# A two-layer trunk kernel on one core: some weight tiles of layer 0 go into the matmul as loaded, in float32

## The chip, the core and the metric

The kernel runs on 1 core of one Trainium2 chip. The metric is the device time in microseconds (us) of one execution; the median of 3 runs of the kernel before is 559.33 us (558.77 to 559.34). Float32 data reaches TensorE in two forms here: as `float32` (called plain below), and as `float32r`, a rounded form. The kernel gets its precision from pairs of `float32r` tiles: a tile `hi` that holds the rounded value and a tile `lo` that holds the rest.

## The reference, cut to what matters

Input: 256 tokens of width 1024, float32. Each of two layers computes

```
h = rmsnorm(x, pre_g) * (1 + scale) + shift      # scale, shift, gate from silu(c) @ ada_w + ada_b
y = concat(branch_i(h) * silu(z_i)) @ out_w
x = x + gate * rmsnorm(y, post_g)
```

In layer 0 `h @ in_w` gives z (2048 columns), the channels of a state space branch (SSD, behind a causal convolution of 4 taps), 16 step sizes, and q, k, v of 16 attention heads. The output projection takes 2048 rows of weights to 1024 columns. Layer 1 has the same frame with other branches. The change touches two places of layer 0: the products of h with the weights of z, and the last 256 of the 2048 rows of the output projection.

## The kernel before, in words

Weights come in units of 1 MB, 128 x 2048 values, in the order that `stream_order` (L42) writes down: eight pieces of modulation, between them seven units called x (the convolution channels and the first unit of z), then for layer 0 seven more units of z, 4 of v, 8 of qk and 8 of the output projection. Behind z1, z3, z5 and z7 stands one more 1 MB piece each (a "gate" piece, consumed by VectorE into `acc`); pieces of the next layer's modulation stand behind some units of qk and of the output projection.

A unit lands in one of 3 buffers called `raw`. Each of its halves (128 x 1024) is split by `next_half` (L900): ScalarE writes `whi`, and VectorE or, where the planner prefers it, GpSimd writes `wlo = raw - whi`. There are 4 buffers of each. After both splits `raw` is free for the next load. `proj_cm` (L921) multiplies a half in three terms of 8 matmuls, 256 columns wide: hi by hi, hi by lo, lo by hi, against `hhi` and `hlo`, the two parts of h. So a half of z is 24 matmuls, a unit 48.

`hhi` and `hlo` come from `xnT`, which holds h in plain float32 after `h0_rows` (L1289) has modulated it in place. `xnT` lies in the only buffer of tag `D`; in the kernel before nobody reads it after that, and the next tiles in that buffer are `dtw_` (L1342, work space for the step sizes, 16 partitions by 7 rows), then `vt` (v of layer 0), then others.

While the z units are multiplied, other engines work on what stands beside them: the convolution (`conv`: ScalarE and VectorE), softplus of the step sizes, the SSD branch (`cb_group`, `x_tokens`, `ssd`), and the gate pieces.

`out_proj` (L995) goes over 16 row tiles r of 128 rows. Row tile r takes half of a weight unit and the matching activation tile, which `ysplit` (L990) has split into `yh` and `yl` for two row tiles at a time; these lie in tag `r2`, which has 5 buffers of 512 columns. Each row tile makes 3 terms by 2 column parts of 512, for the token half m = 0, and the same again for m = 1. For r below `FIRST_HELD` (10) both halves follow each other; from r = 10 on the m = 1 products are kept for later ("held"), so that `residual(0, 0, ...)` (L1029) can begin when all rows of m = 0 are done, and its result feed `make_h1` (L961) and the first three v units of layer 1, which are multiplied half by half (`NV = 3`). Held rows 10 and 11, and the two halves of the first v unit, have their split tiles in buffers of tag `A` (11 buffers of 1024 columns) in place of `whi` and `wlo`.

The order of the work is not the order of the source. `Plan` records every operation, and `schedule` (L502) simulates a list of priorities with cost figures of its own and tries 120 variations with a fixed random seed; `issue` then emits the best order found, for all engines. Each engine executes its own instructions in that order. A changed operation can therefore change the order of operations far from it. Since all operations are emitted by one helper, the profile puts them all on one line, L535, and they are told apart by their tiles: `mm<-hhi,whi` is a product of a half's hi tile with hhi.

Of the kernel before, what the change touches and what calls it, by code (L numbers as in the profile page):

```python
# [15 lines left out]
SEQ = 256  # L16
DM = 1024
KT = 8
# [599 lines left out]
def trunk(ctx, tc, par, s5par, x, w, dtw, fw, postg, gateb, out):  # L618
    nc = tc.nc
    plan = Plan()  # L620
    V, A, G, T, S = (plan.engine(n, e) for n, e in (
        ("DVE", nc.vector), ("ACT", nc.scalar), ("POOL", nc.gpsimd), ("PE", nc.tensor), ("SP", nc.sync)))
# [5 lines left out]
    def const(shape, name, dt=F32):  # L628
        return plan.fixed(sb.tile(shape, dt, name=name))
# [14 lines left out]
    def shaped(t, shape):  # L644
        n = 1
        for d in shape[1:]:
            n *= d
        t = t[0:shape[0], 0:n]
        if len(shape) == 3:
            t = t.rearrange("p (a b) -> p a b", b=shape[2])  # L650
        elif len(shape) == 4:
            t = t.rearrange("p (a b c) -> p a b c", b=shape[2], c=shape[3])
        return t

    def tmp(tag, shape):
        return shaped(plan.new(tags[tag]), shape)

    def rows_of():

        made = {}  # L660

        def row(i, n=None):
            q, j = divmod(i, 4)
            if q not in made:
                made[q] = tmp("A", [P, 4, SEQ])
            return made[q][:, j, :] if n is None else made[q][:, j:j + n, :]
        return row

    def tmp_rounded():
        return plan.new(tags["A"], R32, tags["whi"].slots[0])  # L670

    def bank(tag):
        return plan.new(banks[tag])
# [28 lines left out]
    def pc(name, a=0, b=None):  # L702
        lo, hi = PCOLS[name]
        return pt[:, lo + a:(hi if b is None else lo + b)]
# [42 lines left out]
    for n in range(2):  # L747
        k, pb = slice(4 * n, 4 * n + 4), bank("st")
# [19 lines left out]
    def softplus(xb, tmps):  # L768

        e, s, s2, p = tmps  # L770
        V.scalar_tensor_tensor(e, xb, -1.0, xb, op0=ALU.mult, op1=ALU.min)
        A.activation(e, e, AF.Exp)
        V.tensor_scalar(s2, e, 2.0, None, op0=ALU.add)
        V.reciprocal(s2, s2)
        V.tensor_mul(s, e, s2)
        V.tensor_mul(s2, s, s)
        V.tensor_scalar(p, s2, 1.0 / 15.0, None, op0=ALU.mult)
        for c in (13, 11, 9, 7, 5, 3):
            V.scalar_tensor_tensor(p, p, 1.0 / c, s2, op0=ALU.add, op1=ALU.mult)
        V.scalar_tensor_tensor(p, p, 1.0, s, op0=ALU.add, op1=ALU.mult)  # L780
        V.tensor_scalar(e, xb, 0.0, None, op0=ALU.max)
        V.scalar_tensor_tensor(e, p, 2.0, e, op0=ALU.mult, op1=ALU.add)
        return e

    def split(src, hi, lo, lo_eng=None):
        A.activation(hi, src, AF.Copy)
        if lo_eng:
            lo_eng.tensor_sub(lo, src, hi.bitcast(F32))
        else:
            sub2(lo, src, hi.bitcast(F32))  # L790
# [60 lines left out]
    at = [0, 0]  # L851
# [18 lines left out]
    def modulation(i):  # L870

        while stream[i][0] in ("mod", "gate"):
            if i not in modulated:
                modulated.add(i)
                kind, l, c, *kh = stream[i]
                if kind == "mod":
                    if l == 0:
                        plan.rank = c - 500.0
                    modulate(l, c, load(i)[0:2])
                    if l == 0:  # L880
                        h0_rows(c)
                    plan.rank = None
                else:
                    ada_piece(l, c, kh[0], load(i)[2])
                    if kh[0] == 1:
                        ada_done(l, c)
            i += 1
        return i

    def raw_half():  # L890
        if at[1] == 0:
            raw_half.halves = load(at[0])
        return raw_half.halves[at[1]]

    def step():
        at[1] += 1
        if at[1] == 2:
            at[0], at[1] = at[0] + 1, 0

    def next_half(kdim, spare=False):  # L900

        at[0] = modulation(at[0])
        hi, lo = (tmp_rounded(), tmp_rounded()) if spare else (tmp("whi", [P, 1024]), tmp("wlo", [P, 1024]))
        it = stream[at[0]]
        split(raw_half(), hi, lo, G if it[0] == "x" and 2 * it[1] + at[1] in POOL_X else None)
        step()
        return [t.rearrange("p (k n) -> p k n", k=kdim) for t in (hi, lo)]

    def mm3(o, terms, first=True, last=True, **kw):

        for t, pairs in enumerate(terms):
            with plan.together():
                for j, (a, b) in enumerate(pairs):
                    T.matmul(o, a, b, start=first and t == 0 and j == 0,
                             stop=last and t == 2 and j == len(pairs) - 1, **kw)

    def by_terms(s_hi, s_lo, m_hi, m_lo, ks):

        return [[(a(k), b(k)) for k in ks] for a, b in ((s_hi, m_hi), (s_hi, m_lo), (s_lo, m_hi))]

    def proj_cm(done):  # L921

        pb = bank("mm").rearrange("p (m t) -> p m t", m=2)
        for m in range(2):
            hi, lo = next_half(KT)
            mm3(pb[:, m, :], by_terms(*(lambda k, t=t: t[:, k, :] for t in (hi, lo, hhi, hlo)), range(KT)))
        done(pb)
# [62 lines left out]
    def ysplit(ysrc):  # L990
        yh, yl = tmp("r2", [P, 2, SEQ]), tmp("r2", [P, 2, SEQ])
        split(ysrc, yh, yl)
        return yh, yl

    def out_proj(l, ytile):  # L995


        acc = [[bank("mm"), bank("mm")], [bank("mm"), bank("mm")]]
        ys = {}

        def rows(r, hl, m, parts=((0, 512), (512, 1024))):
            hi, lo = hl
            yh, yl = ys[r // 2]
            c = slice(P * m, P * m + P)
            for t, (a, b) in enumerate(((yh, hi), (yh, lo), (yl, hi))):
                with plan.together():
                    for c0, c1 in parts:
                        n, o = divmod(c0, 512)
                        T.matmul(acc[m][n][:, o:o + c1 - c0], a[:, r % 2, c], b[:, 0, c0:c1],
                                 start=(r == 0 and t == 0), stop=(r == 15 and t == 2), skip_group_check=True)  # L1010


        held, first = {}, FIRST_HELD[l]
        for r in range(16):
            if r % 2 == 0:
                ys[r // 2] = ysplit(ytile(r // 2))
            hl = next_half(1, l == 0 and r in HELD_A)
            rows(r, hl, 0)
            if r < first:
                rows(r, hl, 1)  # L1020
            else:
                held[r] = hl
        x0 = residual(l, 0, acc[0])
        for c in ((0, 512), (512, 1024)):
            for r in range(first, 16):
                rows(r, held[r], 1, (c,))
        return x0, residual(l, 1, acc[1])
# [100 lines left out]
    def silu_to(dst):  # L1128
        def done(pb):
            A.activation(dst, pb, AF.Silu)  # L1130
        return done
# [126 lines left out]
    xnT = tmp("D", [P, KT, SEQ])  # L1258
    for m in range(2):
# [8 lines left out]
        for q in range(2):  # L1268
# [3 lines left out]
            pb = bank("st")  # L1272
            with plan.together():
                for j in range(4):
                    k = 4 * q + j
# [5 lines left out]
    for i, n in enumerate(NWARM2):  # L1281
        m, q = divmod(i, 2)
# [35 lines left out]
    zs = rows_of()  # L1318
    for n in range(14):
# [3 lines left out]
        hi, lo = next_half(8)  # L1323

        for run in ([[0, 1], [2, 3], [4, 5], [6, 7]] if n >= 12 else [range(8)]):
            for t, (a, b) in enumerate(((hi, hhi), (hi, hlo), (lo, hhi))):
                with plan.together():
                    for j in run:
                        k, c = items[j]
                        T.matmul(xb6[c // 2][:, c % 2, :], a[:, j, :], b[:, k, :],  # L1330
                                 start=(k == 0 and c % 2 == 0 and t == 0), stop=(k == 7 and t == 2),
                                 skip_group_check=True)
# [6 lines left out]


    pdt = proj_small(0, "st")
    dtw_ = tmp("D", [16, 7, SEQ])  # L1342
    xb, adtT = dtw_[:, 0, :], dtw_[:, 5:7, :]
    aneg = const([16, 1], "aneg")
    A.activation(xb, pdt[1], AF.Copy)
    V.scalar_tensor_tensor(xb, pdt[0], pc("dtb")[0:16], xb, op0=ALU.add, op1=ALU.add)
    A.activation(aneg, pc("alog")[0:16], AF.Exp)
    spv = softplus(xb, [dtw_[:, n, :] for n in range(1, 5)])
    V.tensor_copy(adtT[:, 0, :], spv)
    V.tensor_scalar(adtT[:, 1, :], spv, aneg, -1.0, op0=ALU.mult, op1=ALU.mult)  # L1350
    dtk = const([P, 2, 2, 16], "dtk")
# [113 lines left out]
            5: [lambda: ssd(0)], 7: [lambda: ssd(1)], 9: [lambda: ssd(2)], 11: [lambda: ssd(3)]}  # L1465
    for i in range(8):
        if i:
            proj_cm(silu_to(zs(2 * i, 2)))
        for f in side.get(i, ()):
            f()  # L1470
    for i in range(4):
# [5 lines left out]
    for i in range(8):  # L1477
        proj_cm(qkdone(i, vt, zs(8 + i)))
        if i == 0:
            ssd_norm()  # L1480
            s5_prepare()
# [9 lines left out]
    for m in range(2):  # L1491
        make_h1(m, xns[m])
        c = slice(P * m, P * m + P)
        for n in range(NV):
            for t, kh in ((0, 0), (1, 0), (0, 1), (1, 1), (2, 0), (2, 1)):
                if (n, kh) not in vw:
                    vw[n, kh] = next_half(4, 2 * n + kh in V_A)
                h, w_ = ((hhi, 0), (hhi, 1), (hlo, 0))[t]
                with plan.together():
                    for k in range(4):  # L1500
                        T.matmul(vb[n][:, m, :], h[:, 4 * kh + k, c], vw[n, kh][w_][:, k, :],
                                 start=(m == 0 and t == 0 and kh == 0 and k == 0), stop=(t == 2 and kh == 1 and k == 3),
                                 skip_group_check=True)
# [18 lines left out]
    xb = ft[:, 0, :]  # L1522
# [3 lines left out]
    spv = softplus(xb, [ft[:, n, :] for n in range(1, 5)])  # L1526
# [134 lines left out]


FIRST_HELD = (10, 12)
HELD_A, V_A = (10, 11), (0, 1)

NWARM = 14
# [104 lines left out]
```

## Time and profile before

| | before |
|---|---|
| median of 3 runs | 559.33 us |
| the profiled execution's own time | 557.83 us |
| its span (first to last instruction) | 556.1 us |
| mean granted TensorE clock | 0.974 |
| busy: TensorE, VectorE, ScalarE, GpSimd | 521.6, 480.5, 366.9, 99.2 us |

A busy time is the sum of the instructions' records. A matmul's record is longer than what it costs in a row of matmuls, since they are pipelined: two records overlap. So what a matmul costs is read from the distance between starts, and an idle stretch is only the time in which no record runs. The granted clock is given as a share of 2.4 GHz; 0.5 would be 1.2 GHz.

### The profile page before, as it was taken

The page shows a single profiled execution, that of the slowest core. Times are in us where ns is not written, and L with a number is a line of the kernel's source. Part 1 is how long each engine was busy: PE and PEld are TensorE (multiplying, and loading weights), DVE is VectorE, ACT ScalarE, POOL GpSimd, SP SyncE. Part 2 cuts the span into 40 slices and gives each one's busy share as a digit, 9 for nine tenths or more (in the row PEclk, how much of TensorE's full clock was granted, in tenths as well). Part 3 has the DMA queues.
Part 4 walks back from the last instruction along what each step waited for, and adds up shares of the span by engine and source line. Part 5 has one row for each costly group of instructions (what it writes and reads, how often), then busy time and mean ns, then how long its engine had stood idle before and what let it go on. Part 6 is the DMA issues. An engine that isn't in the chain of part 4 may idle for free.

```text
span 556.1 us, 10554 instructions
## 1 busy us (share of the span) xinstructions
PE 521.6 (94%) x3996; PEld 467.7 (84%) x3996; DVE 480.5 (86%) x1077; ACT 366.9 (66%) x761; POOL 99.2 (18%) x97
## 2 busy tenths in 40 slices
PE   6999889899999999999599999999999879999995
PEld 4899878899989897778499998999989648887784
DVE  7898899999999999884947989999999775977974
ACT  5644883776576787555746477676767877877731
POOL 5300213224043000004200101112254410000000
PEclk9899989999999999999799999999999969999999
DMA  8999428457442277886305263335454310374812
GB/s 308 410 407 366 154 81 289 161 187 269 152 147 83 82 303 299 314 324 268 151 1 210 94 246 136 150 102 203 162 188 159 122 55 1 99 265 170 331 48 75
DMA packets 18626, 105.27 MB, mean 189 GB/s; under 512 B 2064, under 2 KB 2704, under 8 KB 8336
## 3 DMA queue, kind: packets, MB, share of 16 engines
q1 hardware_dynamic: 18576, 104.60, 50.7%
q8 instruction: 31, 0.51, 0.4%
q14 instruction: 19, 0.16, 0.1%
HBM read 103.55 MB, written 1.05 MB: 188 GB/s over the span
## 4 chain that ended last, share of the span: by engine, by line
PE 68%; DVE 17%; ACT 8%; issue 4%; DMA 1%; SPq 0%; POOLq 0%; POOL 0%; DVEq 0%; ACTq 0%
PE mm L535 52%; PE st L535 11%; PE y L535 5%; DVE b L535 5%; DVE wlo L535 4%; ACT whi L535 3%; DVE st L535 2%; ACT b L535 2%; DVE a L535 2%; DMA A<-in_w_dram 1%; DVE tb L535 1%; ACT A L535 1%; ACT L535 1%; ACT a L535 1%; DVE acc L535 1%
## 5 line engine op out<-in xcount | busy, mean ns | idle before, releaser
L535 ACT ACTIVATE whi<-raw 128x1024 fp32r<-128x1024 f32 x124 | 128.5, 1054 | 60.9 <-PE mm L535 47.1
L535 DVE TENSOR_TENSOR wlo<-raw,whi 128x1024 fp32r<-128x1024 f32 x107 | 132.1, 1246 | 21.1 <-ACT whi L535 20.8
L535 PE MATMUL mm<-hhi,whi 128*128 128x256 f32 x664 | 94.1, 282 | 5.0 <-ACT whi L535 4.0
L535 PE MATMUL mm<-hlo,whi 128*128 128x256 f32 x664 | 93.7, 281 | 0.0
L535 PE MATMUL mm<-hhi,wlo 128*128 128x256 f32 x656 | 93.0, 282 | 0.0
L535 PEld LDWEIGHTS mm<-hhi,whi 128*128 128x128 f32 x664 | 84.4, 189 | 7.6 <-ACT whi L535 4.7
L535 PEld LDWEIGHTS mm<-hlo,whi 128*128 128x128 f32 x664 | 84.2, 188 | 2.8 <-issue 2.5
L535 PEld LDWEIGHTS mm<-hhi,wlo 128*128 128x128 f32 x656 | 83.0, 188 | 3.3 <-issue 3.1
L535 ACT ACTIVATE b<-b,s 128x128 f32<-128x128 f32 (+1 forms) x160 | 65.8, 446 | 18.6 <-DVE s L535 18.2
L535 PE MATMUL mm<-whi,r 128*128 128x512 f32 x240 | 67.7, 394 | 0.0
L535 POOL TENSOR_TENSOR wlo<-raw,whi 128x1024 fp32r<-128x1024 f32 x17 | 41.6, 2455 | 102.9 <-ACT whi L535 97.1
L535 PEld LDWEIGHTS mm<-whi,r 128*128 128x128 f32 x240 | 44.3, 188 | 10.1 <-issue 1.2
L535 ACT ACTIVATE b<-tb,s5r 128x64 f32<-128x64 f32 (+3 forms) x128 | 41.0, 383 | 7.2 <-DVE tb L535 5.0
L535 PE MATMUL mm<-wlo,r 128*128 128x512 f32 x120 | 38.9, 394 | 0.6 <-DVE wlo L535 0.6
L535 DVE CUSTOM_DVE_ANT_0 raw<-raw,condb 128x1024 f32<-128x1024 f32 x32 | 38.2, 1217 | 0.4 <-DMA raw<-in_w_dram 0.4
L535 POOL TENSOR_TENSOR s<-s,nhalf 128x1 f32<-128x1 f32 (+1 forms) x9 | 7.8, 863 | 109.0 <-DVE s L535 107.1
L535 PEld LDWEIGHTS mm<-wlo,r 128*128 128x128 f32 x120 | 22.1, 188 | 5.8 <-DVE wlo L535 1.0
L535 DVE CUSTOM_DVE_ANT_0 b<-st,amask 128x128 f32<-128x128 f32 (+1 forms) x80 | 24.1, 351 | 1.6 <-PE st L535 1.4
L535 ACT ACT_TABLE_LOAD x16 | 20.5, 1283 | 6.0 <-DVE a L535 4.9
L535 DVE TENSOR_TENSOR tb<-b 128x16 f32<-128x16 f32 (+3 forms) x110 | 19.9, 219 | 4.3 <-ACT b L535 3.8
L535 PE MATMUL mm<-wlo,hhi 128*128 128x256 f32 x144 | 23.2, 283 | 0.1
L535 PE MATMUL mm<-whi,hhi 128*128 128x256 f32 x144 | 23.0, 281 | 0.0
(238 smaller groups left out, 896.7 us busy)
## 6 DMA issues: line engine op xcount, KB each, us to landing
raw<-in_w_dram SPq DMA_DIRECT2D x80, 1024.0 KB, 4.9
raw<-in_w_dram SPq DMA_DIRECT2D x16, 512.0 KB, 10.2
A<-in_w_dram SPq DMA_DIRECT2D x14, 512.0 KB, 10.2
xres<-in_x_dram SPq DMA_DIRECT2D x2, 512.0 KB, 4.3
b<-in_gateb_dram SPq DMA_DIRECT2D x4, 256.0 KB, 6.2
b<-in_postg_dram SPq DMA_DIRECT2D x4, 256.0 KB, 6.2
out_dram<-xres SPq DMA_DIRECT2D x3, 256.0 KB, 2.0
A<-in_s5par_dram SPq DMA_DIRECT2D x1, 512.0 KB, 5.7
```

The lines of the kernel that those rows point to most:

```text
L535: getattr(self.engines[e], method)(*[at(v) for v in a], **{n: at(v) for n, v in k.items()})
```

## The change

For z units 1, 3, 5 and 7 (`PLAIN_Z`), `proj_cm` gets h in plain float32 and takes the weights from `raw` without a split: one term of 8 float32 matmuls for a half. `raw` is read by the matmuls themselves, and so is in use until they end; `xnT` is in use until z7 is done. For row tiles 14 and 15 of layer 0 (`PLAIN`, the entry 16 leaves layer 1 as it was), `out_proj` takes the activation tile without `ysplit`, the weights from `raw`, and one term. `dtw_` moves to two buffers of tag `A`.

```diff
+    def raw_next():
+
+        at[0] = modulation(at[0])
+        r = raw_half()
+        step()
+        return r
...
-    def proj_cm(done):
+    def proj_cm(done, h=None):
...
+            if h is not None:
+                wt = raw_next().rearrange("p (k n) -> p k n", k=KT)
+                with plan.together():
+                    for k in range(KT):
+                        T.matmul(pb[:, m, :], wt[:, k, :], h[:, k, :], start=(k == 0), stop=(k == KT - 1))
+                continue
...
-            hi, lo = hl
-            yh, yl = ys[r // 2]
             c = slice(P * m, P * m + P)
-            for t, (a, b) in enumerate(((yh, hi), (yh, lo), (yl, hi))):
+            if r >= PLAIN[l]:
+                terms = ((ys[r // 2], hl[:, None, :]),)
+            else:
+                (yh, yl), (hi, lo) = ys[r // 2], hl
+                terms = ((yh, hi), (yh, lo), (yl, hi))
+            for t, (a, b) in enumerate(terms):
...
-                ys[r // 2] = ysplit(ytile(r // 2))
-            hl = next_half(1, l == 0 and r in HELD_A)
+                ys[r // 2] = ytile(r // 2) if r >= PLAIN[l] else ysplit(ytile(r // 2))
+            hl = raw_next() if r >= PLAIN[l] else next_half(1, l == 0 and r in HELD_A)
...
-    dtw_ = tmp("D", [16, 7, SEQ])
-    xb, adtT = dtw_[:, 0, :], dtw_[:, 5:7, :]
+    dtw_ = [tmp("A", [16, 4, SEQ]) for _ in range(2)]
+    xb, adtT = dtw_[0][:, 0, :], dtw_[1][:, 1:3, :]
...
-            proj_cm(silu_to(zs(2 * i, 2)))
+            proj_cm(silu_to(zs(2 * i, 2)), xnT if i in PLAIN_Z else None)
...
+PLAIN_Z = (1, 3, 5, 7)
+PLAIN = (14, 16)
```

## Rows read from the trace of the kernel before

**Rows 1.** The table of stretches, one row each (from two such tables): stretch, length, then busy time and count of PE, PEld, DVE, ACT and POOL, the granted clock, the DMA share and GB/s.

```profile
58.50:68.00 9.50, 9.15 (x77) 8.94 (x76) 7.12 (x15) 9.36 (x17) 2.40 (x1) 1.00 0.46 163
68.00:80.00 12.00, 8.34 (x68) 8.11 (x69) 11.71 (x25) 11.94 (x23) 2.47 (x1) 1.00 0.36 135
80.00:90.00 10.00, 10.00 (x70) 9.47 (x70) 9.79 (x25) 3.89 (x7) 0.00 (x0) 0.83 0.46 165
90.00:100.00 10.00, 7.59 (x63) 7.19 (x62) 9.96 (x14) 5.02 (x9) 6.02 (x7) 1.00 0.77 257
...
56.80:121.33 64.53, 57.96 (x477) 55.11 (x475) 61.33 (x107) 46.54 (x72) 15.30 (x12) 0.97 0.50 180
121.33:152.00 30.67, 30.67 (x255) 29.68 (x256) 29.73 (x60) 19.53 (x31) 7.29 (x6) 1.00 0.58 206
152.00:222.00 70.00, 69.17 (x575) 60.80 (x574) 64.87 (x204) 53.07 (x136) 11.34 (x14) 1.00 0.48 179
222.00:264.40 42.40, 41.80 (x190) 33.48 (x188) 30.55 (x43) 23.80 (x34) 6.28 (x3) 1.00 0.79 301
264.40:273.90 9.50, 2.65 (x13) 2.31 (x13) 8.90 (x22) 7.14 (x20) 3.49 (x6) 0.68 0.58 222
```

**Rows 2.** TensorE's timeline where it stood idle in the z stage: start, length, the group, and in brackets the idle time before it and what ended it.

```profile
69.37 2.24 PE L535 MATMUL mm<-hhi,whi 128*128 128x256 f32 x16 [1.72 <-ACT whi L535]
...
79.50 1.58 PE L535 MATMUL mm<-hhi,whi 128*128 128x256 f32 x8 [2.29 <-ACT whi L535]
80.88 2.76 PE L535 MATMUL st<-A 128*128 128x256 f32 x8
83.30 1.28 PE L535 MATMUL mm<-hhi,wlo 128*128 128x256 f32 x8
...
98.86 0.76 PE L535 MATMUL st<-ident,A 128*128 128x128 f32 x5 [2.41 <-ACT A L535]
```

**Rows 3.** TensorE's groups of instructions between 56.8 and 121.33 us, shapes kept apart: count, busy time, mean ns.

```profile
L535 PE MATMUL mm<-hhi,whi 128*128 128x256 f32 x118 | 17.3, 287 | 4.0 <-ACT whi L535 4.0
L535 PE MATMUL y<-b,A 128*64 128x128 f32 x48 | 3.1, 277 | 0.0
```

**Rows 4.** TensorE's timeline, the first 8 of 24 float32r matmuls of 256 columns in a row (z stage) and what follows the 24, then of 512 columns (output projection).

```profile
93.15 1.10 PE L535 MATMUL mm<-hhi,whi 128*128 128x256 f32 x8
...
95.95 0.49 PE L535 MATMUL st<-ident,A 128*128 128x128 f32 x3
...
247.93 2.88 PE L535 MATMUL mm<-A,r 128*128 128x512 f32 x12
250.65 0.61 PE L535 MATMUL mm<-whi,r 128*128 128x512 f32 x2
```

**Rows 5.** TensorE's timeline, matmuls of plain float32: the first of 32 records of the S5 branch in layer 1 (on `y`, four column strips of 32 at a time), and what comes after the last.

```profile
379.43 0.64 PE L535 MATMUL y<-D,s5c 128*32 128x256 f32 x8
...
381.30 0.75 PE L535 MATMUL mm<-wlo,hhi 128*128 128x256 f32 x4
```

**Rows 6.** The page's groups: the costs of a split, and of the weight loads beside the matmuls (their means); then the weight loads of the plain float32 group of rows 2, from PEld's timeline.

```profile
L535 ACT ACTIVATE whi<-raw 128x1024 fp32r<-128x1024 f32 x124 | 128.5, 1054 | 60.9 <-PE mm L535 47.1
L535 DVE TENSOR_TENSOR wlo<-raw,whi 128x1024 fp32r<-128x1024 f32 x107 | 132.1, 1246 | 21.1 <-ACT whi L535 20.8
L535 PEld LDWEIGHTS mm<-hhi,whi 128*128 128x128 f32 x664 | 84.4, 189 | 7.6 <-ACT whi L535 4.7
...
80.67 2.68 PEld L535 LDWEIGHTS st<-A 128*128 128x128 f32 x8
```

**Rows 7.** The SP queue in the z stage (start, length of the stretch of issues, how many), and the time from issue to landing.

```profile
59.56 23.15 SPq L535 DMA_DIRECT2D raw<-in_w_dram  x4
82.76 0.42 SPq L535 DMA_DIRECT2D A<-in_s5par_dram  x1
88.51 3.48 SPq L535 DMA_DIRECT2D raw<-in_w_dram  x2
...
raw<-in_w_dram SPq DMA_DIRECT2D x80, 1024.0 KB, 4.9
```

**Rows 8.** The split of the last activation tiles in the output projection: ScalarE writes `yh` of rows 14 and 15, and GpSimd writes their `yl`.

```profile
248.62 0.61 ACT L535 ACTIVATE r<-A 128x512 fp32r<-128x512 f32 x1
258.82 1.29 POOL L535 TENSOR_TENSOR r<-A,r 128x512 fp32r<-128x512 f32 x1 [1.99 <-PE mm L535]
```

**Rows 9.** TensorE's timeline at the end of the output projection (`A` tiles are the weights of the held rows 10 and 11) and the start of layer 1.

```profile
253.82 0.62 PE L535 MATMUL mm<-wlo,r 128*128 128x512 f32 x2
254.27 1.52 PE L535 MATMUL mm<-A,r 128*128 128x512 f32 x6
...
257.44 1.52 PE L535 MATMUL mm<-A,r 128*128 128x512 f32 x6
...
271.28 2.99 PE L535 MATMUL st<-ident,A 128*128 128x128 f32 x12 [6.86 <-DVE A L535]
273.93 1.53 PE L535 MATMUL mm<-A,hhi 128*128 128x256 f32 x8
275.29 0.63 PE L535 MATMUL mm<-whi,hhi 128*128 128x256 f32 x4
```

**Rows 10.** The same stretch on ScalarE (the first square of the residual) and in the chain of waits (start, length, what).

```profile
262.20 0.60 ACT L535 ACTIVATE b<-mm 128x512 f32<-128x512 f32 x1 [0.50 <-PE mm L535]
...
265.06 0.10 DVE wlo L535
265.16 1.00 issue
...
268.30 0.06 DVE wlo L535
268.36 0.99 issue
```

More of the change, by code (lines that the diff above doesn't have):

```diff
@@ L1009, in rows @@
                         T.matmul(acc[m][n][:, o:o + c1 - c0], a[:, r % 2, c], b[:, 0, c0:c1],
-                                 start=(r == 0 and t == 0), stop=(r == 15 and t == 2), skip_group_check=True)
+                                 start=(r == 0 and t == 0), stop=(r == 15 and t == len(terms) - 1),
+                                 skip_group_check=True)
         held, first = {}, FIRST_HELD[l]
@@ L1347, in trunk @@
     A.activation(aneg, pc("alog")[0:16], AF.Exp)
-    spv = softplus(xb, [dtw_[:, n, :] for n in range(1, 5)])
+    spv = softplus(xb, [*(dtw_[0][:, n, :] for n in range(1, 4)), dtw_[1][:, 0, :]])
     V.tensor_copy(adtT[:, 0, :], spv)
```

## The prediction

> **What bounds the kernel now.** I read the table of stretches first, because the share of TensorE over the whole span (94%) says nothing of a stage. From 58.5 to 100 us, where the z units are multiplied, the row to look at is the one with an engine at its full length: ScalarE 11.94 of 12 us from 68 to 80, VectorE 11.71 of 12, 9.79 of 10 and 9.96 of 10 [rows 1]. TensorE has gaps there, and the granted clock falls to 0.83 in one row. TensorE's timeline names the gaps: 1.72 and 2.29 us until ScalarE had written a `whi`, 2.41 us until a Silu of the convolution had passed ScalarE [rows 2]. So this stage is bound by the two engines that split weights and do the side work. From 121 to 264 us it is the other way round: 141.6 us of records in 143.1 us [rows 1]; TensorE is the bound and a microsecond of its work is a microsecond of time. Then comes the largest single gap of layer 0: 6.86 us before the first transposes of layer 1, with the clock at 0.68 around it [rows 1, 9].
>
> How much of the z stage is gap? I count what TensorE had to do between 56.80 and 121.33 us, at the spacing of starts. Of float32r matmuls of 256 columns there are 385 (118 in each of the three terms on `mm`, 31 others), and 24 of them take 2.80 us from 93.15 to 95.95, so 0.1167 each: 44.9 us [rows 3, 4]. The two SSD groups (48 records) take 2.9 at 1.46 a group, 16 transposes 1.8, 14 float32r matmuls of 512 columns 3.3, the plain float32 group of rows 2 half of its 2.42 us, small ones 0.5. Sum 54.6 in 64.5 us: 9.9 us are gaps, slow clock and the starts of groups. The three named gaps are 6.4 of it, the slow clock near 81 us about 1.7.
>
> **The change in z.** Eight halves lose 24 float32r matmuls each, 192 x 0.1167 = 22.4 us, and get 8 plain ones each, 64 in all. What a plain float32 matmul of 256 columns costs at full clock is not in the trace for a full array, so I bound it. The S5 group shows 32 records for 16 such matmuls, two records each, four strips side by side: 379.43 to 381.30 is 1.87 us for 8 in a row, 0.234 a record, 0.468 a matmul [rows 5]. The group on `A` in rows 2 has a full array: two matmuls of 256 columns and two of 128, worth three of 256, from 80.88 to 83.30, so 0.807 each at the low clock (1.2 GHz), 0.403 at the high one. A record of plain float32 streams as long as a float32r record of twice its columns, and 512 columns of float32r cost 2.72 / 12 = 0.227 [rows 4]; that is the nearest row, and I take 0.228 a record, 0.456 a matmul. 64 x 0.456 = 29.2, so TensorE gets +6.8 us (+3.4 to +7.5).
>
> What goes is 8 splits: 8 x 1.05 us of ScalarE and, mostly on VectorE, 8 x 1.25 us [rows 6]. That is worth nothing by itself, only through the 9.9 us. I expect most of the gaps to close. The first two waits are for a `whi` on a ScalarE that is full from 58.5 to 80; z1 and z3 then need no ScalarE at all and TensorE can take them while z2 and z4 are split. The third gap stands behind a VectorE that had been full since 68 us; by then it is some 6 splits lighter. With the plain units TensorE needs 54.6 + 6.8 = 61.4 us in this stage, VectorE 61.3 - 8 = 53 [rows 1], so TensorE becomes the bound, and what is late next is its own work. About 1 us of the 9.9 is the starts of groups and stays. I take 7.0 recovered (0 to 9). Behind 121 us TensorE was the bound already, so lighter splits give nothing there.
>
> Three side effects in z I cost at zero. `raw` is now held until the matmuls end, not until the split: a 1 MB load lands 4.9 us after its issue, and only six `raw` loads were issued from 59.56 to 92 us [rows 7], so there is time between them for a unit of 7.3 us; if the cover is gone, z3, z5 and z7 wait up to 4.9 us each, 14.7 in all. SP issues in order, so whatever is queued behind a load that waits for a `raw` buffer is late with it: the gate's bias tiles and the next unit. `xnT` held until z7 delays only `vt`, whose first writer comes after v0, itself behind z7: nothing, or a fraction of a us if the order is changed. `dtw_` in two `A` buffers is gone at about 89 us and can only push back the load of the S5 parameters at 82.76 [rows 7], for which nobody waits until attention begins; a gain I exclude, since nothing waited for the old place.
>
> **The change in the output projection.** 24 float32r matmuls of 512 columns (5.44 us at 0.2267) become 8 plain ones. Two records of 512 columns cost at most twice 0.456 and at least twice 0.403; I take 0.89: 7.1 us, so +1.7 (+1.0 to +1.9), on the path, because TensorE is the bound there.
>
> The removed `ysplit` is worth more than its 1.9 us. Tag `r2` has 5 buffers; rows 10 to 13 hold four until their m = 1 products are done, `yh` of rows 14 and 15 took the fifth at 248.62, and `yl` was written only at 258.82, after a wait for TensorE [rows 8]: the held rows 10 and 11 had to go first, at 254.27 and 257.44 [rows 9]. So the m = 0 products of rows 14 and 15 ended near 262.2, where the first square of the residual starts [rows 10]. Without `ysplit` they can follow row 13. By 254.27 row 14 had its two `yh` terms (0.91 us); so m = 0 ends at 254.3 - 0.9 + 4 x 0.88 = 256.9, 5.3 us earlier. The held work then lasts 24 x 0.227 + 3.5 = 8.9 us, to 265.8. The residual's chain took 262.20 to 271.28, 9.1 us, of which 1.00 + 0.99 was VectorE splitting weights of layer 1 ahead of it [rows 10]. From 256.9 it ends at 264.0 to 266.0, under the held products. Then TensorE has the m = 0 part of three v units (72 x 0.118 = 8.5 us, plus transposes 0.9), to 275.2, while the m = 1 chain runs from 265.8 to 272.9 or 274.9; the transposes of m = 1 and the new h may leave a gap of up to 2.2. Before, 6.86 us of idle and about 1.8 of slow clock stood here (12 transposes in 2.65 us, and 8 matmuls in 1.36 where 0.93 is usual [rows 9]): 8.6 in all, of which I take 6.4 (2.0, the two splits alone, to 8.6). This also asks of two `whi` buffers that rows 14 and 15 no longer hold: they let the second v unit be split before the residual starts.
>
> **The sum.** +6.8 - 7.0 + 1.7 - 6.4 = -4.9 us. On the profiled execution's 557.83 us that is 552.9; this execution lies 1.5 below the median of the runs, so against 559.33 I predict 554.4. The layer 1 order is planned anew too, which may move a microsecond either way; I add nothing for it.
>
> **A rule against it.** Weight loads show a mean of 189 ns, yet the float32r matmuls that need one each start every 117 ns, and the 8 loads of the plain group took 2.68 us beside matmuls of 2.42 [rows 2, 4, 6]: loads run under the matmul before them. If they did not for plain float32, each of the 128 + 16 records would cost up to 0.189 more, 27 us: 557.83 + 22 = about 580, 581 by the median. The Trainium skill, "TensorE: Matmul & The Clock Gate", section Part 3: Packing small matmuls, states that a load overlaps matmuls in flight only when its row group differs, which full-array matmuls would not satisfy. By that rule the time is the 581; the trace disagrees, with 117 ns under 189.
>
> **Rivals.** (1) Slower: `raw` becomes the bound in z. Every plain unit keeps its buffer through 7.3 us of TensorE, with three buffers for z and gate units; z3, z5 and z7 then wait on average 2.3 us for their load and the 7.0 are not recovered: +6.8 + 1.7 - 6.4 = +2.1, 561.4. For it: SP has its issues bunched with long pauses, so buffers are what it waits for. Against: ScalarE and VectorE are what TensorE waited for, never a load [rows 2]. It decides the sign once less than 2.1 of the 9.9 us come back. (2) No change: the planner keeps held products ahead of the last m = 0 rows, so the end of layer 0 gains the two splits only: +6.8 - 7.0 + 1.7 - 2.0 = -0.5, 558.8. For it: the order is found by search, not by this argument; against: the wait that forced it [rows 8] no longer exists. (3) Faster than I say: plain matmuls near 0.427, all 9 us of z and all 8.6 of the end: +4.9 - 9 + 1.4 - 8.6 = -11.3, 548. (4) Weight loads not hidden, above, 581.
>
> **How the numbers follow.** Forecast 0.58, (1) 0.15, (2) 0.12, (3) 0.12, (4) 0.03. The range goes from 549 to 561.5: it takes in (2) and (1) and most of the way to (3), and leaves out (4). About 0.2%, 1.1 us, is what a measurement of this kernel tells from no change. Faster: forecast and (3), 0.70. Same: (2), 0.12. Slower: (1) and (4), 0.18.
>
> **What would show it.** In z: plain groups of 16 records on `mm` about 3.65 us apart, no waits of TensorE for `whi` between 60 and 100 us, VectorE no longer full there. If waits for a load of `raw` stand there, (1) is right. At the end of layer 0: the residual's first square some 9 us before the last held product, no gap of 6.9 us, a clock near 1. If that gap stands and the square starts within 2 us of the last product, (2). A record spacing well above 0.234 us would be (4). Wrong in any case would be an unchanged sum of gaps in both places.

## The result and the profile after

The changed kernel takes 543.48 us (median of 4 runs, 542.59 to 546.29) against 559.22 us: a ratio of 0.9737, 95% interval 0.971 to 0.9763, 15.7 us less. The forecast was 554.4 us with a range from 549 to 561.5. The direction was right; the gain is three times the forecast, and the time lies outside the range. The profiled execution took 542.97 us with a span of 541.2 (556.1 before).

The table of stretches of the changed kernel, columns as in [rows 1]:

```profile
60.00:80.00 20.00, 19.45 (x115) 17.70 (x115) 19.57 (x43) 16.78 (x28) 0.00 (x0) 1.00 0.42 158
80.00:100.00 20.00, 19.54 (x131) 17.87 (x129) 18.31 (x33) 9.57 (x15) 2.73 (x2) 1.00 0.71 254
100.00:115.00 15.00, 14.85 (x98) 13.08 (x99) 14.68 (x30) 5.93 (x12) 3.02 (x3) 1.00 0.59 215
115.00:148.00 33.00, 33.00 (x287) 31.73 (x285) 32.12 (x77) 24.91 (x35) 7.66 (x5) 1.00 0.53 196
148.00:210.00 62.00, 62.00 (x537) 55.94 (x537) 57.00 (x172) 47.16 (x121) 6.95 (x11) 1.00 0.53 191
210.00:259.10 49.10, 49.10 (x222) 36.84 (x220) 38.89 (x66) 27.18 (x49) 1.09 (x2) 1.00 0.73 274
259.10:279.00 19.90, 19.09 (x158) 18.68 (x158) 15.31 (x45) 13.66 (x34) 4.21 (x4) 1.00 0.30 106
```

The first busy time in a row is TensorE's: it has records nearly all the time from 60 to 259 us, and the clock is 1.00 in every row, where [rows 1] has 0.83 near 85 us and 0.68 before layer 1. The third is VectorE's: it is still almost full in z. So a full engine in the table is not yet the bound; what TensorE waits for is.

TensorE's timeline of the changed kernel: plain units (`mm<-D,raw`) among the float32r ones in z, then the end of layer 0, where `mm<-raw,A` is rows 14 and 15. In brackets the idle time before a group.

```profile
60.05 7.07 PE L535 MATMUL mm<-D,raw 128*128 128x256 f32 x32
66.77 1.29 PE L535 MATMUL mm<-hhi,whi 128*128 128x256 f32 x8
67.89 1.10 PE L535 MATMUL mm<-hlo,whi 128*128 128x256 f32 x8
...
72.34 3.72 PE L535 MATMUL mm<-D,raw 128*128 128x256 f32 x16 [0.56 <-DMA raw<-in_w_dram]
...
100.15 0.73 PE L535 MATMUL st<-r,onesr 128*128 128x512 f32 x2 [0.61 <-DVE A L535]
...
240.93 2.88 PE L535 MATMUL mm<-A,r 128*128 128x512 f32 x12
...
246.38 3.59 PE L535 MATMUL mm<-raw,A 128*128 128x512 f32 x8
249.41 1.94 PE L535 MATMUL mm<-A,r 128*128 128x512 f32 x6
251.18 0.39 PE L535 MATMUL mm<-whi,r 128*128 128x512 f32 x1
...
257.48 1.88 PE L535 MATMUL mm<-raw,A 128*128 128x512 f32 x4
259.10 0.75 PE L535 MATMUL mm<-A,hhi 128*128 128x256 f32 x4
...
270.07 1.32 PE L535 MATMUL mm<-A,hhi 128*128 128x256 f32 x8 [0.81 <-ACT hhi L535]
...
279.00 1.09 PE L535 MATMUL mm<-hhi,whi 128*128 128x256 f32 x8
```

The three waits of [rows 2] are gone; from 60 to 115 us two short ones are left, one of them for a load of `raw`. The m = 0 products of rows 14 and 15 now follow row 13 and end near 249.4, ahead of the held rows 10 and 11 at 249.41, and layer 1 starts at 259.10 without the 6.86 us of [rows 9]. ScalarE's row of the residual's first square answers to [rows 10]; it stands 10 us before layer 1 starts:

```profile
249.15 0.60 ACT L535 ACTIVATE b<-mm 128x512 f32<-128x512 f32 x1 [2.72 <-PE mm L535]
```

**Reading by segments.** The order is searched anew for each kernel, so one total says little of one edit. I cut every span at three points that mark the same work in all kernels: the first `y` matmul of the x stage, the first m = 0 group of rows 10 and 11 (`mm<-A,r`), and the first u group of layer 1 (the products of the weight units u, which follow the first three v units; `mm<-hhi,whi`, 279.00 above). TensorE has the same number of matmul records in each segment of every kernel here, but for the plain terms, so equal work is compared: counted by their starts, 1702 in the z segment (1638 with four plain units), 232 at the end of layer 0 (224 with plain rows), 1964 in layer 1. Before and after:

| us | start | z segment | end of layer 0 | layer 1 | span |
|---|---|---|---|---|---|
| before | 23.67 | 224.26 | 43.96 | 264.2 | 556.1 |
| after | 22.02 | 218.91 | 38.07 | 262.2 | 541.2 |
| difference | -1.7 | -5.3 | -5.9 | -2.0 | -14.9 |

Start and layer 1, whose operations the change does not touch, hold 3.7 us of it. That was the question for the later runs.

The z segment as one stretch, before and after, columns as in [rows 1]:

```profile
23.67:247.93 224.26, 216.25 (x1705) 198.88 (x1704) 209.12 (x459) 149.80 (x277) 35.57 (x34) 0.99 0.61 229
...
22.02:240.93 218.91, 217.75 (x1640) 198.89 (x1639) 203.76 (x464) 142.25 (x268) 21.32 (x22) 1.00 0.65 243
```

TensorE is idle for 8.0 us before and 1.2 after. VectorE is busy for 93% of the segment in both; of the work that went, 14.3 us went from GpSimd, 7.6 from ScalarE and 5.4 from VectorE, since the planner gives splits to GpSimd too.

### The profile page after: what moved, and what is told of

Read it like the earlier page. It is cut to its first block, busy times and chain, and to the rows that moved or that the text cites. A ratio compares the mean times of both kernels' runs of the same rounds, so it can differ in the third digit from the quotient of the medians.

```text
span 541.2 us, 10376 instructions
## 1 busy us (share of the span) xinstructions
PE 521.1 (96%) x3924; PEld 464.5 (86%) x3924; DVE 474.5 (88%) x1091; ACT 354.4 (65%) x745; POOL 72.2 (13%) x75
## 4 chain that ended last, share of the span: by engine, by line
PE 75%; DVE 11%; ACT 6%; DMA 4%; issue 2%; SPq 0%; POOL 0%; POOLq 0%; DVEq 0%; ACTq 0%
PE mm L535 58%; PE st L535 12%; PE y L535 6%; DVE wlo L535 3%; DVE b L535 3%; DMA raw<-in_w_dram 2%; ACT b L535 2%; DVE st L535 2%; ACT whi L535 2%; DMA A<-in_w_dram 1%; DVE tb L535 1%; ACT A L535 1%; DVE a L535 1%; DVE D L535 1%; ACT L535 0%
## 5 line engine op out<-in xcount | busy, mean ns | idle before, releaser
L535 ACT ACTIVATE whi<-raw 128x1024 fp32r<-128x1024 f32 x114 | 118.6, 1054 | 57.6 <-PE mm L535 36.9
L535 DVE TENSOR_TENSOR wlo<-raw,whi 128x1024 fp32r<-128x1024 f32 x101 | 123.7, 1238 | 14.6 <-ACT whi L535 14.5
L535 PE MATMUL mm<-hhi,whi 128*128 128x256 f32 x600 | 85.0, 282 | 2.2 <-ACT qk L535 2.2
L535 PE MATMUL mm<-hlo,whi 128*128 128x256 f32 x600 | 85.0, 282 | 0.0
L535 PE MATMUL mm<-hhi,wlo 128*128 128x256 f32 x592 | 83.8, 282 | 0.0
L535 PEld LDWEIGHTS mm<-hlo,whi 128*128 128x128 f32 x600 | 75.8, 188 | 2.7 <-issue 2.7
L535 POOL TENSOR_TENSOR wlo<-raw,whi 128x1024 fp32r<-128x1024 f32 x13 | 31.5, 2430 | 88.1 <-ACT whi L535 86.8
L535 PE MATMUL mm<-D,raw 128*128 128x256 f32 x128 | 28.7, 380 | 0.6 <-DMA raw<-in_w_dram 0.6
L535 DVE CUSTOM_DVE_ANT_0 b<-st,amask 128x256 f32<-128x256 f32 (+1 forms) x80 | 24.2, 352 | 3.8 <-PE st L535 3.6
L535 PEld LDWEIGHTS mm<-D,raw 128*128 128x128 f32 x128 | 23.9, 190 | 3.8 <-DMA raw<-in_w_dram 0.8
```

The source lines that it names most:

```text
L535: getattr(self.engines[e], method)(*[at(v) for v in a], **{n: at(v) for n, v in k.items()})
```

## The experiments

**The two parts alone, and neither.** Edits of the changed kernel's settings:

```diff
-PLAIN = (14, 16)              # e1_z_only
+PLAIN = (16, 16)
...
-PLAIN_Z = (1, 3, 5, 7)        # e2_out_only
+PLAIN_Z = ()
```

and both for the third.

> Only the z units 1, 3, 5, 7 plain; the output projection as before. Theory A (two independent gains: z worth 4.8 us, end of layer 0 worth 6.3 us, some 2 us either way from the order being searched anew): about 554.5 us, no wait for whi above 1 us in z, and the gap of about 6.9 us before layer 1 still there. Theory B (the new order alone, or the moved dtw_, gives most of it): no more than 2 us from the kernel with neither. Theory C (all of it is the z stage, since lighter ScalarE and VectorE also clear the end): about 545.

> Only row tiles 14 and 15 of the output projection plain. Theory A: about 553 us, the gap before layer 1 under 2 us and the residual's first square some 9 us before the last held product; the gaps of 6.4 us in z stay. Theory B: within 2 us of the kernel with neither. Theory C: about 559, or 561 with the added work of TensorE.

> The changed source with both settings empty: only dtw_ lies in two A buffers, and the order is searched anew. Theory A: 559 us, within 2. Theory B: 550 or less. Theory C: 559.

Measured: z alone 557.81 us (ratio 0.9972, 0.9954 to 0.999), the projection alone 552.18 (0.9877, 0.9841 to 0.9913), neither 559.39 (1.0015, 0.9993 to 1.0037). Neither is as theory A has it: the moved `dtw_` costs nothing. The projection alone fits A: the gap before layer 1 is gone and the waits in z stay. z alone does not (and of the gap of 6.9 us that A wanted to see, 5.0 stand there): by its total it looks like B, and 7.0 + 1.3 us are far from the 15.7 of both. The segments resolve it:

| us | start | z segment | end of layer 0 | layer 1 |
|---|---|---|---|---|
| neither | 22.87 | 226.68 | 43.88 | 264.2 |
| z alone | 24.63 | 219.24 | 44.89 | 267.7 |
| projection alone | 21.01 | 226.66 | 37.80 | 265.4 |
| both (the change) | 22.02 | 218.91 | 38.07 | 262.2 |

In its own segment each part does the same alone and together, some 7.5 us in z and 6 at the end of layer 0. What hid the gain of z alone was a start 2.6 and a layer 1 5.5 us longer than in the changed kernel.

**The fifth r2 buffer.** A sixth buffer of `r2` would be the plainest test, but there is no room for it: the tiles would take 208.97 KB of a partition and 207.87 are left. So that variant has no time. Instead: the kernel before, nothing plain, only the place of one tile changed:

```diff
-        yh, yl = tmp("r2", [P, 2, SEQ]), tmp("r2", [P, 2, SEQ])
+        yh = tmp("r2", [P, 2, SEQ])
+        yl = shaped(tmp_rounded(), [P, 2, SEQ]) if spare else tmp("r2", [P, 2, SEQ])
...
-                ys[r // 2] = ysplit(ytile(r // 2))
+                ys[r // 2] = ysplit(ytile(r // 2), l == 0 and r == 14)
```

> The kernel before, nothing plain; only yl of rows 14 and 15 lies in a buffer of tag A in place of the fifth r2 buffer that it had to wait for. Read by segments, from the start of the m = 0 products of rows 10 and 11 to the first u matmul of layer 1 (43.96 us before, 38.07 after). If the fifth buffer was what kept rows 14 and 15 back: yl follows its yh within 2 us, the gap before layer 1 falls below 3 us, the segment is 37 to 39 us, and the time about 553 us, 3 either way from the new order elsewhere. If it is the whi buffers that plain rows give back, or the missing splits: the segment stays above 42 us.

Measured: 553.94 us (0.9914, 0.988 to 0.9948), end of layer 0 38.64 us. Rows of VectorE's timeline (`yl` of rows 14 and 15) and ScalarE's (`yh`, and the first square), then all idle rows of TensorE from 249 to 290 us:

```profile
251.72 0.68 DVE L535 TENSOR_TENSOR A<-A,r 128x512 fp32r<-128x512 f32 x1
```

```profile
248.95 0.63 ACT L535 ACTIVATE r<-A 128x512 fp32r<-128x512 f32 x1 [0.40 <-PE mm L535]
...
257.56 0.60 ACT L535 ACTIVATE b<-mm 128x512 f32<-128x512 f32 x1 [2.25 <-PE mm L535]
```

```profile
267.41 1.21 PE L535 MATMUL mm<-A,hhi 128*128 128x256 f32 x8 [0.83 <-ACT hhi L535]
270.78 1.22 PE L535 MATMUL mm<-A,hhi 128*128 128x256 f32 x8 [0.40 <-ACT hhi L535]
279.23 1.20 PE L535 MATMUL mm<-A,hhi 128*128 128x256 f32 x8 [1.16 <-ACT hhi L535]
```

`yl` follows its `yh` after 2.8 us where [rows 8] has 10.2 (I had said 2), and of the gap 2.4 us in three pieces are left. So one wait for one buffer is worth nearly the whole net gain at the end of layer 0; plain matmuls are one way to be rid of it and another address for one tile is another. They are not the same inside: plain rows leave 0.8 us of gap where this leaves 2.4, and pay for it with 1.4 us more of TensorE.

**Old split work given back.** The plain halves of z are split all the same:

```diff
         r = raw_half()
+        if stream[at[0]][0:3] == ("in", 0, "z"):
+            split(r, tmp("whi", [P, 1024]), tmp("wlo", [P, 1024]))
         step()
```

> The changed kernel, but the 8 plain halves of z are also split into whi and wlo tiles that nobody reads, so ScalarE and VectorE have their old work and TensorE the new one. If the gain in z came through the lighter ScalarE and VectorE: the segment from the first y matmul of the x stage to the rows 10 and 11 (224.3 us before, 218.9 after) goes to 224 us or above, 549 to 552 us in all. If it came from TensorE alone (the plain units need no split to have been done before them): within 2 us of 218.9, about 544.

Measured: z segment 228.38 us, end of layer 0 38.24, layer 1 271.4, in all 560.16 (1.0015, 0.9991 to 1.0039). TensorE's waits from 60 to 130 us (total, times, longest):

```profile
PE mm L535 <- DVE wlo L535: 4.2, 4, 1.8
PE mm L535 <- DMA raw<-in_w_dram: 1.3, 1, 1.3
PE mm L535 <- ACT whi L535: 0.8, 1, 0.8
...
```

The z segment as one stretch:

```profile
21.62:250.00 228.38, 221.44 (x1641) 200.02 (x1639) 212.87 (x463) 148.00 (x273) 36.40 (x34) 0.99 0.62 232
```

With the splits back, TensorE waits for splits again, and the z segment is 9.5 us longer than in the changed kernel, even longer than before: it then has the price of the plain matmuls without what they buy. ScalarE, VectorE and GpSimd have about the work of before, and TensorE is idle for 6.9 us. The gain in z comes through the splits. The edit gives back the use of `whi` and `wlo` buffers together with the engines' time, so these two are not told apart. The total missed its figure by 8 us, again in layer 1.

**Other orders.** `SEED` of the search set to 3, 4 and 5, nothing else.

> The changed kernel with the planner's random seed 3 in place of 2: same operations, another order. Theory A (the two parts are worth some 5 to 7 us and 6 us whatever the order, the start and layer 1 are luck): z segment 218 to 221, end segment 37.5 to 39.5, the start 21 to 25 and layer 1 262 to 268 us; 541 to 550 in all. If the start and layer 1 are faster because of the change: 22 and 262 again, 543.

> The kernel before with seed 3. Theory A: z segment 223 to 228, end segment 43 to 45, the start and layer 1 anywhere in 21 to 25 and 262 to 268: 553 to 562 in all. If the order's luck can by itself give what the change gave: below 549.

> The changed kernel with the planner's seed 4. z segment 216 to 220, end segment 37.5 to 39. If layer 1 is luck: 262 to 271 us of it, 541 to 552 in all. If both parts of the change together shorten layer 1 too: 262 to 264 again, 541 to 544.

> The kernel before with seed 4. z segment 223 to 228, end segment 43 to 45. Layer 1, from the first u matmul to the end, took 264.2 and 266.6 us with seeds 2 and 3, against 260.7 to 263.7 in three orders of the changed kernel. If this is luck of the order: now and then 263 or less here too. If the change shortens layer 1: 264 to 268.

> The kernel before with seed 5; as for seed 4: 263 or less in layer 1 speaks for luck, 264 to 268 for an effect of the change.

> The changed kernel with seed 5. z segment 216 to 220, end segment 37.5 to 39. If layer 1 is luck: anywhere from 261 to 271. If the change shortens it: 260 to 264 once more.

| us | start | z segment | end of layer 0 | layer 1 | median |
|---|---|---|---|---|---|
| before, seed 3 | 22.77 | 226.52 | 44.23 | 266.6 | 561.81 |
| before, seed 4 | 22.67 | 223.11 | 44.70 | 265.1 | 557.87 |
| before, seed 5 | 24.55 | 225.10 | 45.13 | 263.4 | 559.54 |
| changed, seed 3 | 23.13 | 216.90 | 38.24 | 263.7 | 543.08 |
| changed, seed 4 | 24.18 | 218.19 | 38.14 | 260.7 | 544.13 |
| changed, seed 5 | 23.44 | 218.30 | 38.00 | 268.7 | 548.65 |

Over the four seeds (2 to 5) the z segment falls from 224.75 to 218.08 in the mean, by 6.7 us, and the end of layer 0 from 44.51 to 38.11, by 6.4; no order of the one kernel reaches the other's values. Start (23.4 and 23.2) and layer 1 (264.8 and 263.8) overlap. Three segments missed the figures set for them (216.90, 45.13 and 260.7), none by more than 1.3 us. After seed 4 a shortening of layer 1 by the change looked likely; seeds 5 of both kernels speak against it. So 13.1 us belong to the change; the other 2.6 of the measured 15.7 are not shown to be its work, and start and layer 1 scatter by more than that.

The same split shows in TensorE's idle time in the z segment. In the seven kernels here without plain z units it is 7.1 to 9.7 us, with a mean granted clock of 0.970 to 0.992; in the nine with plain units and without their splits it is 0.0 to 1.4 us, with 1.000.

Where layer 1 gets longer is seen from the table of stretches, 40 us of attention at the same distance from the first u group (140 to 180 us), first the changed kernel, then the one with all z units plain (below), which was 8.9 us longer in layer 1:

```profile
419.00:459.00 40.00, 34.75 (x292) 27.69 (x292) 30.37 (x101) 31.45 (x93) 6.69 (x9) 0.91 0.16 54
```

```profile
421.30:461.30 40.00, 35.53 (x262) 26.52 (x263) 29.51 (x92) 30.47 (x86) 13.87 (x15) 0.83 0.30 106
```

TensorE's busy time is alike, but 262 matmuls are done in place of 292 and the clock is lower: the second has two waits for ScalarE of 2.4 us in this stretch, and the granted clock is 0.5 behind each; the first has one such stretch, behind a wait of 3.4 us. Over all of layer 1 the same 1964 records fill 257.0 us in the second against 249.5, and 1.4 us more are idle.

Whether this is luck alone stays open. Layer 1 takes 263.4 to 266.6 us in the seven kernels without plain z units, and 260.7 to 271.4 in the ten with them, five of these above 267. No run shows why it scatters more there.

**How many units.** `PLAIN_Z` set to (1, ..., 7) and to (1, 3, 5).

> All seven z units plain (1 to 7), the rest as in the changed kernel. If the z stage of the changed kernel is bound by TensorE, three more plain units add 3 x 1.3 us of it and close nothing: z segment 221 to 223 us (218.9 with four), 545 to 549 in all. If splits still bound it: 216 or less.

> Only z units 1, 3 and 5 plain. If three units give ScalarE and VectorE enough air: TensorE saves 1.3 us, z segment about 217 to 218 us. If the gaps come back with the fourth unit's splits: 220 to 223. Layer 1 and the start as luck has it, 541 to 550 in all.

Measured: all seven 551.91 us (0.9888, 0.9861 to 0.9915), z segment 220.91; three 544.07 (0.9743, 0.9727 to 0.9759), z segment 217.54. Against the mean of 218.1 with four units, seven cost 2.8 us more, near what their added TensorE work does (3.9), and three are no worse. TensorE is idle for 0.0 us of the z segment with seven and 0.8 with three. So at four units z is bound by TensorE. The total with seven lies above its figure, by layer 1.

**Towards a faster version.** The z part with `yl` in a buffer of tag A in place of plain rows; and the change with `ROUNDS = 480`.

> z units 1, 3, 5, 7 plain, the output projection in float32r as before, but yl of rows 14 and 15 in a buffer of tag A. If the plain rows of the projection did nothing but remove the wait for the fifth r2 buffer: z segment 217 to 219, end segment 37 to 38.6 (1.4 us of TensorE saved, two more splits in the way), 541 to 548 in all.

> The changed kernel with 480 variations in the search in place of 120, for a faster version. If the search still finds shorter orders: 538 to 542 us. If its own cost figures are what limits it: 542 to 546, as with 120.

Measured: 552.63 us (0.9897, 0.988 to 0.9914), with z segment 218.09 and end of layer 0 38.80, both as the changed kernel within a microsecond, and 269.4 in layer 1, by which the total misses its figure; and 545.17 (0.9718, 0.9674 to 0.9762). Neither is clearly faster than the changed kernel. Four times the search found nothing better on the chip in this one run; that its own cost figures limit it would fit, but is not shown.

## Why the prediction was wrong

Term by term (price in z, recovered in z, price and recovered at the end of layer 0) the forecast was +6.8 - 7.0 + 1.7 - 6.4 = -4.9 us. Over four orders the runs showed +5.2 - 11.9 + 1.4 - 7.8 = -13.1.

**The price in z** was right in kind and too high: +6.8 forecast. 32 records take 60.05 to 66.77, and the next float32r group is 0.19 longer than usual: 6.91 / 16 = 0.432 us a matmul, 64 of them 27.6, so +5.2. The term was sized from a float32r matmul of 512 columns (0.227 us): plain records of 256 columns follow each other after 0.216 us, not 0.228.

**"I take 7.0 recovered"** is the step that failed most. With +5.2 paid and 6.7 gained in the mean, about 11.9 us came back, more than the 9.9 I had counted as the ceiling. The count ended at 121.33 us and took the rest as bound by TensorE ("lighter splits give nothing there"), but two waits behind it went too:

```profile
162.48 0.55 PE L535 MATMUL st<-ident,b 128*128 128x128 f32 x3 [0.80 <-ACT b L535]
...
243.22 0.74 PE L535 MATMUL mm<-wlo,r 128*128 128x512 f32 x2 [0.60 <-DVE wlo L535]
```

In the pair of the table, idle fell by 6.8 us in this segment and the slow clock gave some 1.7: 8.5 of the 10.5 that came back there, and the other 2 are not named. Over the four seeds idle fell by 7.2 in the mean (7.8 to 0.6), and the clock, 0.98 in the mean before and 1.000 after, is worth an estimated 4.2: 11.4 of the 11.9. So the order that the prediction read had less slow clock in z than the other three, and its ceiling of 9.9 was lower than what they had to give. The mechanism (splits set the pace of z, plain units relieve them) was right and is shown by the run that gave the splits back. That VectorE would no longer be full was wrong: the segment got shorter with its work.

**The end of layer 0** came out by its own steps: the missing `ysplit` lets rows 14 and 15 of m = 0 go first, shown apart from plain matmuls by the run with `yl` elsewhere. Forecast -6.4 + 1.7 = -4.7; measured -6.4 net in the mean. The added work is 3.03 + 0.41 = 3.44 us for the four m = 0 matmuls, 0.86 each, 6.88 for eight, so +1.4. So 7.8 us came back of the 8.6 that stood there, not 6.4: only 0.81 us of gap is left, where I had allowed 2.2.

**"A microsecond either way"** for the new order was far too small: equal work of TensorE took 260.7 to 271.4 us in layer 1 and 21.0 to 24.6 at the start. The range should have had some 4 us more on both sides for it alone.

**The rivals.** (1) `raw` as the bound: SP did wait 9.8 us from 58 to 116 us for plain matmuls to free a buffer, but one wait of 0.56 us for a load is all that reached TensorE, so it fell. (2) The order at the end followed the freed buffer: the segment is 37.8 to 38.8 us in every run that freed it, 43.9 to 45.1 in the others. (4) Weight loads of plain matmuls show a mean of 190 ns, the same as float32r's, in the changed kernel's groups from 56 to 122 us:

```profile
L535 PE MATMUL mm<-D,raw 128*128 128x256 f32 x128 | 28.7, 380 | 0.6 <-DMA raw<-in_w_dram 0.6
L535 PEld LDWEIGHTS mm<-D,raw 128*128 128x128 f32 x128 | 23.9, 190 | 3.8 <-DMA raw<-in_w_dram 0.8
```

They lie wholly beside matmul records that start every 0.216 us. The rule of the Trainium skill, "TensorE: Matmul & The Clock Gate", section Part 3: Packing small matmuls, that a load overlaps matmuls in flight only in another row group, would, as an estimate, have put 0.190 us on top of each; these full-array matmuls disagree. (The same section also lets a load into a background weight buffer go ahead.) (3) came nearest, by the size of what closed: it had -11.3 us.

## What to carry to other kernels

Where float32 precision is made of three float32r products, taking some tiles as plain float32 trades about a quarter more TensorE time in them (0.432 us for three times 0.1167) for the whole split work; it pays while TensorE waits for splits, and three or four units of seven were enough here. Before a costly remedy at a stage's end, look for the one buffer that a late tile waits for: another address for it gave the same here without a change in the arithmetic. And where an order is searched anew for every edit, compare segments at marks of equal work, over several seeds; by totals alone the z part was worth 1.3 us in one pair, while its own segment shows 5.0 in that pair and 6.7 over four seeds.

## What the runs showed of the hardware that was not expected

A plain float32 matmul of 256 columns on the full array costs 0.432 us at a granted clock of 1.00, two records 0.216 apart; 512 columns cost 0.86. Against float32r's 0.1167 and 0.2267 that is a factor of 3.7 and 3.8, not the 3.9 that I had taken. The end of a plain group is to be read with care: the next float32r group has its first start 0.03 us behind the last plain one, and takes 0.19 us longer for its first 8 matmuls, so starts counted up to it alone would give 0.420 a matmul.
